# A hybrid mLSTM and sparse-attention block on one core: new pacing of background work, shared banks for turned tiles, part of the weight splits on GpSimd, and an interleaved tail

## The chip, the cores and the metric

The kernel runs on one core of a Trainium2 chip, as one launch. The metric is the time of the program on the device in microseconds. The engines are named as the profile names them: PE is TensorE, DVE is VectorE, ACT is ScalarE, POOL is GpSimd, SP is the engine that issues most DMAs.

## The reference

One decoder block on x of 512 tokens by 1024 channels, in float32:

```
u    = rmsnorm(x, norm_in)
proj = u @ w_in                                  # 1024 x 6736, split into the parts below
# mLSTM group: 4 heads, q and k 128 wide (conv of 4 taps, SiLU), v 256 wide
hm   = mlstm(q, k, v, log_i, log_sigmoid(f));  hm = rmsnorm per head * m_norm
hm   = sigmoid(m_o) * hm * silu(m_z)
# attention group: 8 heads of 64; an indexer's score picks the 128 best keys of each query
score[t, s] = sum_h w[t, h] * relu(iq[t, h] . ik[s]),  s <= t;  idx = top_k(score, 128)
ha   = softmax(aq . ak / 8 + rel_bias, over idx) @ av * silu(a_z)
h    = x + concat(hm, ha) @ w_out                # 1536 x 1024
h    = h + (p @ w_ple) * sigmoid(h @ w_ple_gate) # 256 x 1024 and 1024 x 1024
out  = rmsnorm(h, norm_final)
```

## The kernel before

**Products.** Each float32 operand is split into a high part, rounded to the type that PE takes, and a low part, the rest; a product is three matmuls (high by high, high by low, low by high) into one PSUM bank. For weights, `split` (L143) does this: a slab of 1024 elements a partition (two k tiles of 512 columns, or four of 256) is loaded to `raw`, two ACT operations copy its halves to `wh`, and two DVE operations subtract to `wl`. `work` (L156) emits one of these four jobs at a tick and issues the load of a later slab when the last is out; `feed` and `piece` (L164, L172) make sure that a slab is split one slab ahead. Slabs are numbered in the order of `plan`: 36 and 37 are the columns of the first pair of attention heads, 38 to 41 the attention's v (`av`), 42 to 47 the other pairs, 48 to 51 its gate (`az`), 52 to 63 the output projection (`wo`), 64 to 73 the last products.

**Order.** The order of instructions on PE, DVE, ACT and POOL is the order in which the program emits them. A `tick` (L188) follows every step of three matmuls of a dense product. It emits what `later(n, ...)` (L182) put off until now, one weight job, and background work: `back` is a list of generators, and each tick adds 1.0 to a credit from which every piece subtracts the cost that it yields. The background holds, in this order, the indexer's scores (24 pieces, COST_SC), the gate sequences, the convolutions of q and k (COST_CV), and the top-k (48 pairs of MAX8 and MATCH_REPLACE8, L567 and L569, COST_TK a pair); `split_mix` (COST_MX) joins during the mLSTM.

**Stages.** The dense products of q and k take 64 ticks, v 64, the output gates `o` and `z` of half the mLSTM 64. The mLSTM's 32 steps are then woven (L269) with 112 steps of dense products: `gates_oz(1)`, pair 0 of the attention's q and k (`aqk`), and `av`. When the top-k has ended, the attention's 32 units (one head, one tile of 128 queries) are woven with pairs 1 to 3, `az` and most of the output projection's first half. Then come the rest of that projection, the turned residual, and the gate of the per-layer embedding (`wg`).

**PSUM.** Dense products use a ring of four banks ("mm"), everything else a second ring of four ("x"). A tile takes the bank of the tile allocated four before it in its ring, and its first write waits until that one's last reader is done. In the attention a head allocates four logits (`lg_ps`, read by `least`, L801), four turned probability tiles (`pt_ps`, L825, one for each query tile, read by a copy on ACT and a subtraction on DVE), and one product with v (`av_ps`, read last by DVE into `ha`). The turned tiles of units 0 and 1 of a head are made in the same iteration. After pair 0, the four banks of `av` follow those of `z` and of `aqk`: the third takes the query bank, the fourth the key bank, whose four subtractions (`ak2`, L776) come 2 to 5 ticks after its last matmul, the copies (`ak1`, L775) 0 to 3 ticks after it.

**Masks.** The mask of unit k+1 is added one unit ahead (L783): by POOL for all but its last 256 columns, by DVE for those.

**Tail.** `gated` (L964) evacuates a row tile of `wg`: tanh on ACT, two DVE steps that add the gated embedding to `h`, a square on ACT with an accumulated sum. `evac_gate1` (L990) does it for the second half of the columns, in two halves of 256, then the power on POOL, the multiplication by the gain, the scaling on DVE and ACT, and the stores. Row tiles 0 and 1 are made together, then 2, then 3 in two banks:

```
    for i in range(2):
        done = evac_gate1(i, [two[i], two[i]])
        later(2 + 2 * i, finish, done, 0)
        later(3 + 2 * i, finish, done, 1)
    for i in range(2, NT):
        ...
            next(done)
        run(done)
```

Of the kernel before, what the change touches and what calls it, by code (L numbers as in the profile page):

```python
# [16 lines left out]
OP = mybir.AluOpType  # L17
# [3 lines left out]
P = 128  # L21
# [9 lines left out]
DPLE = 256  # L31
EPS = 1e-6
NTMP, NHM, NKEEP = 7, 3, 37
COST_SC, COST_CV, COST_TK, COST_MX, RATE_M, RATE_A = 1.7, 2.0, 2.6, 2.0, 3.5, 3.2
NR, NW, NS = 3, 4, 1
QK0 = 10
POOLW = (0, 1, 2)
# [10 lines left out]
def block_kernel(ctx: ExitStack, tc: tile.TileContext, x, p, w_in, b_gate, conv_w, w_out, norm_in,  # L48
# [30 lines left out]
    def x_bank(name, shape=(P, S)):  # L79
        return pp.tile(list(shape), F32, tag="x", bufs=4, name=name)  # L80
# [4 lines left out]
    def f(ap):  # L85
        return ap.bitcast(F32)
# [56 lines left out]
    def split(k):  # L143

        raw = loaded.pop(k)
        nk, n = raw.shape[1:]
        h = wp.tile([P, KP * S], F32R, tag="wh", bufs=NW, name="wh")[:, 0:nk * n].rearrange("p (k n) -> p k n", n=n)
        l = wp.tile([P, KP * S], F32R, tag="wl", bufs=NW, name="wl")[:, 0:nk * n].rearrange("p (k n) -> p k n", n=n)
        ready[k] = h, l
        halves = [slice(0, nk // 2), slice(nk // 2, nk)]  # L150
        jobs.extend((k, A.activation, (h[:, q, :], raw[:, q, :], AF.Copy)) for q in halves)
        jobs.extend((k, V.tensor_tensor, (l[:, q, :], raw[:, q, :], f(h)[:, q, :], OP.subtract)) for q in halves)

    jobs = []

# [21 lines left out]

    back, credit, clock, due = [], [0.0], [0], []  # L180

    def later(n, fn, *args):  # L182
        heapq.heappush(due, (clock[0] + n, len(order), fn, args))
        order.append(None)
# [3 lines left out]
    def tick():  # L188
        clock[0] += 1
        while due and due[0][0] <= clock[0]:  # L190
            _, _, fn, args = heapq.heappop(due)
            fn(*args)  # L192
        if jobs:
            work()
        credit[0] += 1.0
        while back and credit[0] >= 0.0:
            g = back[0]
            cost = next(g, None)
            if cost is None:
                back.remove(g)  # L200
            else:
                credit[0] -= cost
        if not back:
            credit[0] = 0.0
# [430 lines left out]
    def gates_oz(c):  # L635
        yield from dense_fm(4, evac_o(4 * c), name="o")
        yield from dense_fm(4, evac_z(4 * c), name="z")
# [124 lines left out]
    def evac_aqk(pair):  # L762
        def go(b, ps):
            half = [slice(0, 64), slice(64, 128)]
            for s in range(2):
                h, me, other = 2 * pair + s, half[s], half[1 - s]
                if b == 0:
                    t = aq[h] = keep(f"aq{h}", F32R)
                    later(s, A.activation, t[me, :], ps[me, :], AF.Copy, 0.0, -DH ** -0.5)
                    later(s + 2, V.scalar_tensor_tensor, t[other, :], ps[me, :], -DH ** -0.5, f(t[me, :]),  # L770
                          OP.mult, OP.subtract)
                else:
                    t1, t2 = ak1[h], ak2[h] = keep(f"ak1_{h}", F32R), keep(f"ak2_{h}", F32R)
                    for q, o in enumerate((me, other)):
                        later(2 * s + q, A.activation, t1[o, :], ps[me, :], AF.Copy)  # L775
                        later(2 * s + q + 2, V.tensor_tensor, t2[o, :], ps[me, :], f(t1[me, :]), OP.subtract)  # L776
        return go

    def attention():
# [35 lines left out]
        def turned(t, i):  # L815
            return bass.AP(tensor=t.tensor, offset=t.offset + P * i, ap=[list(t.ap[0]), [3 * P, i + 1], [1, P]])

        def flip(h, i):
            if i == 0:
                pt[h] = [sp.tile([P, SW], F32R, tag=n, bufs=1, name=n) for n in ("sH", "sL")]  # L820
            tH, tL = pt[h]
            pr = prob.pop((h, i))
            ps = x_bank("pt_ps", (P, i + 1, P))
            for j in range(i + 1):
                T.transpose(ps[:, j, :], pr[:, j * P:(j + 1) * P], ident)  # L825
            later(1, A.activation, turned(tH, i), ps, AF.Copy)
            later(2, V.tensor_tensor, turned(tL, i), ps, f(turned(tH, i)), OP.subtract)

        def values(h):
            tH, tL = pt.pop(h)  # L830
# [20 lines left out]
        n = len(units)  # L851
        turns_at, values_at = {}, {}
        for k, (h, i) in enumerate(units):
            turns_at.setdefault(k + (4 if i == 0 else 3), []).append((h, i))
        for h in range(AH):
            values_at[NT * h + 8] = h
        masks(*units[0])
        for k in range(NT * AH + 5):
            if k < n:
                logits(*units[k])  # L860
            if k + 1 < n:
                later(1, masks, *units[k + 1])
            if k in values_at:
                h = values_at[k]
                values(h)
                if h % 2:
                    later(4 if h > 3 else 48 if h == 1 else 24, close, h // 2)
            for h, i in turns_at.get(k, ()):
                flip(h, i)
            yield  # L870


    def attention_in(b):
        return dense_fm(2, evac_aqk(b), name="aqk")
# [18 lines left out]

    tz = load_bias()
    for k, _ in enumerate(gates_oz(0)):
        if k == QK0:
            split_qk(0)
        if k == QK0 + 12:
            decays_load(0, 0)
            decays_load(0, 1)  # L900
        if k == QK0 + 18:
            decays(0, 0)
    weave(mlstm(), chain(gates_oz(1), attention_in(0), dense_tm(u_h, u_l, list(range(KT)), evac_av, name="av")),
          lambda k: RATE_M)
    while not ended[0]:
        tick()
    out0 = project(0)
    weave(attention(), chain(attention_in(1), attention_in(2), attention_in(3), dense_fm(4, evac_az, name="az"),
                             (next(out0) for _ in range(40))), lambda k: RATE_A)
# [51 lines left out]
    gfin = [gf[:, c * S:(c + 1) * S] for c in range(2)]  # L961
    fs = [col(f"fs{i}", 4) for i in range(NT)]

    def gated(i, c, ps, o, n, acc, wait):  # L964

        sg = tmp("sgg", shape=(P, n))
        t = hs[i, c][:, o:o + n]
        A.activation(sg, ps[:, o:o + n], AF.Tanh, scale=0.5)  # L968

        def add():  # L970
            V.scalar_tensor_tensor(sg, sg, 1.0, ple[i, c][:, o:o + n], op0=OP.add, op1=OP.mult)  # L971
            V.scalar_tensor_tensor(t, sg, 0.5, t, op0=OP.mult, op1=OP.add)
            if wait:
                later(2, square)
            else:
                square()

        def square():
            A.activation(sg, t, AF.Square, scale=D ** -0.5, accum_out=acc)

        if wait:
            later(1, add)
        else:
            add()

    def evac_gate0(i, ps):
        gated(i, 0, ps, 0, S, fs[i][:, 0:1], True)
        later(4, V.tensor_tensor, hs[i, 0], hs[i, 0], gfin[0], OP.mult)

    def evac_gate1(i, parts):  # L990

        r = fs[i][:, 3:4]
        for q, ps in enumerate(parts):
            gated(i, 1, ps, q * 256, 256, fs[i][:, 1 + q:2 + q], False)
            if q == 0:
                V.tensor_scalar(r, fs[i][:, 1:2], fs[i][:, 0:1], EPS, op0=OP.add, op1=OP.add)
            yield
        V.tensor_tensor(r, r, fs[i][:, 2:3], OP.add)
        G.tensor_tensor(r, r, neghalf[:, 0:1], OP.pow)
        V.tensor_tensor(hs[i, 1], hs[i, 1], gfin[1], OP.mult)  # L1000
        for q in range(2):
            cs = slice(q * 256, (q + 1) * 256)
            V.tensor_scalar(hs[i, 1][:, cs], hs[i, 1][:, cs], r, None, op0=OP.mult)
            A.activation(hs[i, 0][:, cs], hs[i, 0][:, cs], AF.Copy, scale=r)
            if i == NT - 1:
                nc.sync.dma_start(out[0, i * P:(i + 1) * P, S + q * 256:S + (q + 1) * 256], hs[i, 1][:, cs])
        if i < NT - 1:
            nc.sync.dma_start(out[0, i * P:(i + 1) * P, S:], hs[i, 1])
        nc.scalar.dma_start(out[0, i * P:(i + 1) * P, 0:S], hs[i, 0])
        yield  # L1010

# [17 lines left out]
        T.matmul(ps[:, cs], h_l(kt, i), h[:, kt % KP, cs], start=False, stop=(kt == KT - 1))  # L1029
        tick()  # L1030

    def finish(done, q):
        next(done)
        if q:
            run(done)

    two = [mm_bank(f"wg{i}") for i in range(2)]
    for k0 in range(0, KT, KP):
        for i in range(2):
            for k in range(KP):  # L1040
                gate_step(i, two[i], slice(0, S), k0 + k)
    for i in range(2):
        done = evac_gate1(i, [two[i], two[i]])
        later(2 + 2 * i, finish, done, 0)
        later(3 + 2 * i, finish, done, 1)
    for i in range(2, NT):
        parts = [mm_bank(f"wg{i}_{q}") for q in range(2 if i == NT - 1 else 1)]
        w = S // len(parts)
        done = evac_gate1(i, [parts[0], parts[-1]])
        for q, ps in enumerate(parts):  # L1050
            for kt in range(KT):
                gate_step(i, ps, slice(q * w, (q + 1) * w), kt)
            next(done)
        run(done)


def _bucket_table():
# [32 lines left out]
```

## Time and profile before

| | |
|---|---|
| time, median of 3 runs | 535.02 us (534.21 to 535.66) |
| profiled execution, its own time | 534.46 us |
| its span | 532.7 us |
| busy: PE, DVE, ACT, POOL | 500.9 (94%), 362.2 (68%), 267.2 (50%), 47.8 us (9%) |
| mean granted clock of PE | 0.984 |
| DMA | 52.25 MB, mean 98 GB/s |

The span is the stretch from the first to the last recorded work of the profiled execution; its own time is 1.8 us longer. Busy times are those of each engine's instructions; a busy PE is counted with the modelled ends of pipelined matmuls, so the distance between two starts tells more of its speed than a duration does. The rows of the next section but one give start and duration in microseconds; what stands in brackets is how long the engine had been idle before the instruction, and what released it.

### The profile page before, as it was taken

How to read it: one execution, taken by the hardware profiler on the slowest of the kernel's cores; microseconds unless marked ns; L12 is line 12 of the kernel's file. 1: busy time of each engine (PE TensorE's matmuls, PEld its weight loads, DVE VectorE, ACT ScalarE, POOL GpSimd, SP SyncE). 2: the span in 40 equal slices, each digit the busy share in tenths (PEclk: the TensorE clock that was granted, in tenths of full speed). 3: DMA queues.
4: the chain of work that ended last, by engine and by line, in shares of the span. 5: the costliest groups of instructions: out<-in, count | busy, mean ns of one | idle time of the engine just before them, and what ended most of it. 6: DMA issues, size and time to landing. Idle time of an engine off the chain costs nothing.

```text
span 532.7 us, 6811 instructions
## 1 busy us (share of the span) xinstructions
PE 500.9 (94%) x2370; PEld 409.6 (77%) x2370; DVE 362.2 (68%) x802; ACT 267.2 (50%) x588; POOL 47.8 (9%) x96
## 2 busy tenths in 40 slices
PE   5999999999999999999979999899999999999980
PEld 4887888788788878887868887678888888788770
DVE  1953464987859699879995997886983542715554
ACT  6643656552614245645654577775764332414343
POOL 4400000000000002110111211111110000000011
PEclk9999999999999999999979999999999999999996
DMA  8442553233433133341322212212234533141122
GB/s 263 141 141 53 89 113 103 81 119 119 160 112 119 43 92 113 95 124 46 100 69 79 81 40 80 79 41 79 53 113 153 172 112 111 53 145 41 39 79 79
DMA packets 37281, 52.25 MB, mean 98 GB/s; under 512 B 4156, under 2 KB 16732, under 8 KB 37248
## 3 DMA queue, kind: packets, MB, share of 16 engines
q1 hardware_dynamic: 32192, 45.49, 26.9%
q10 hardware_dynamic: 4960, 6.31, 5.5%
q8 instruction: 18, 0.29, 0.2%
q14 instruction: 15, 0.12, 0.1%
q0 software_dynamic: 96, 0.02, 0.0%
HBM read 48.13 MB, written 3.69 MB: 97 GB/s over the span
## 4 chain that ended last, share of the span: by engine, by line
PE 78%; DVE 11%; ACT 5%; issue 3%; DMA 1%; POOL 1%; SPq 0%; POOLq 0%; ACTq 0%; DVEq 0%
PE wo L256 4%; PE wo L258 4%; PE wo L257 4%; PE mv L257 3%; PE mv L256 3%; PE mv L258 3%; PE o L236 2%; PE o L234 2%; PE o L235 2%; PE z L234 2%; PE z L236 2%; PE z L235 2%; DVE wl L159 2%; DVE ak L192 2%; PE mq L234 1%
## 5 line engine op out<-in xcount | busy, mean ns | idle before, releaser
L159 DVE TENSOR_TENSOR wl<-raw,wh 128x512 fp32r<-128x512 f32 x140 | 92.9, 684 | 13.5 <-ACT wh L159 13.3
L159 ACT ACTIVATE wh<-raw 128x512 fp32r<-128x512 f32 x140 | 83.2, 624 | 16.6 <-DMA raw<-in_w_ple_gate_dram 5.7
L256 PE MATMUL wo<-wh,mixH 128*128 128x512 f32 x96 | 39.4, 410 | 0.0
L258 PE MATMUL wo<-wh,mixL 128*128 128x512 f32 x96 | 37.8, 394 | 0.0
L257 PE MATMUL wo<-wl,mixH 128*128 128x512 f32 x96 | 37.8, 393 | 0.0
L567 DVE MAX8 m<-sc 128x8 f32<-128x256 f32 (+2 forms) x48 | 26.5, 553 | 0.0
L234 PE MATMUL aqk<-uH,wh 128*128 128x512 f32 x64 | 26.5, 413 | 0.0
L236 PE MATMUL o<-uH,wl 128*128 128x512 f32 x64 | 25.5, 399 | 0.9 <-DVE wl L159 0.9
L236 PE MATMUL aqk<-uH,wl 128*128 128x512 f32 x64 | 25.4, 397 | 1.0 <-DVE wl L159 1.0
L569 DVE MATCH_REPLACE8 sc<-m,sc 128x256 f32<-128x256 f32 (+2 forms) x48 | 26.0, 542 | 0.0
L234 PE MATMUL o<-uH,wh 128*128 128x512 f32 x64 | 25.9, 404 | 0.0
L234 PE MATMUL z<-uH,wh 128*128 128x512 f32 x64 | 25.8, 403 | 0.0
L257 PE MATMUL mv<-wl,uH 128*128 128x512 f32 x64 | 25.7, 401 | 0.0
L235 PE MATMUL o<-uL,wh 128*128 128x512 f32 x64 | 25.4, 396 | 0.0
L235 PE MATMUL z<-uL,wh 128*128 128x512 f32 x64 | 25.3, 396 | 0.0
L236 PE MATMUL z<-uH,wl 128*128 128x512 f32 x64 | 25.3, 396 | 0.0
L256 PE MATMUL mv<-wh,uH 128*128 128x512 f32 x64 | 25.3, 395 | 0.0
L235 PE MATMUL aqk<-uL,wh 128*128 128x512 f32 x64 | 25.3, 395 | 0.0
L258 PE MATMUL mv<-wh,uL 128*128 128x512 f32 x64 | 25.1, 393 | 0.0
L809 ACT ACTIVATE pr<-pr,sm 128x128 f32<-128x128 f32 (+3 forms) x32 | 17.9, 560 | 13.9 <-DVE sm L801 13.6
L543 DVE SCALAR_TENSOR_TENSOR sc<-relu,iwt,sc 128x256 f32<-128x256 f32 (+2 forms) x21 | 13.0, 617 | 15.7 <-ACT relu L192 15.4
L971 DVE SCALAR_TENSOR_TENSOR sgg<-sgg,ple 128x256 f32<-128x256 f32 (+1 forms) x12 | 6.1, 508 | 23.6 <-ACT sgg L968 23.4
(244 smaller groups left out, 1354.0 us busy)
## 6 DMA issues: line engine op xcount, KB each, us to landing
raw<-in_w_in_dram SPq DMA_DIRECT2D x44, 512.0 KB, 3.5
raw<-in_w_out_dram SPq DMA_DIRECT2D x12, 512.0 KB, 3.5
raw<-in_w_in_dram SPq DMA_DIRECT2D x16, 256.0 KB, 2.9
raw<-in_w_ple_gate_dram SPq DMA_DIRECT2D x8, 512.0 KB, 3.7
x<-in_x_dram SPq DMA_DIRECT2D x8, 256.0 KB, 4.8
xr<-in_x_dram SPq DMA_DIRECT2D x2, 1024.0 KB, 4.9
tdram<-tv ACTq DMA_DIRECT2D x1, 1536.0 KB
tz<-tdram ACTq DMA_DIRECT2D x1, 1024.0 KB
```

What stands on the lines that cost most here:

```text
L159: fn(*args)
L192: fn(*args)
L234: T.matmul(banks[b][:, 0:nt], h[:, k, bs], uH[:, kt, tok0:], start=(kt == 0), stop=False)
L235: T.matmul(banks[b][:, 0:nt], h[:, k, bs], uL[:, kt, tok0:], start=False, stop=False)
L236: T.matmul(banks[b][:, 0:nt], l[:, k, bs], uH[:, kt, tok0:], start=False, stop=(kt == KT - 1))
L256: T.matmul(banks[i], aH(kt, i), h[:, k, :], start=first, stop=False)
L257: T.matmul(banks[i], aH(kt, i), l[:, k, :], start=False, stop=False)
L258: T.matmul(banks[i], aL(kt, i), h[:, k, :], start=False, stop=last)
L543: V.scalar_tensor_tensor(sc, r, w, sc, op0=OP.mult, op1=OP.add)
L567: V.max(out=m8, in_=sel[i])
L569: V.match_replace(out=sel[i], in_to_replace=m8, in_values=sel[i], imm_value=-3e38)
L809: later(2, lambda: A.activation(t, t, AF.Exp, bias=sm[:, 0:1], scale=-1.0, accum_out=sm[:, 1:2]))
```

## The change

- The costs of the background pieces fall: scores 1.7 to 1.2, convolution 2.0 to 1.6, a pair of the top-k 2.6 to 2.0. A tick adds `pace[0]` to the credit instead of 1.0: 1.0 until step 32 of `gates_oz(0)`, 0.6 to the end of it, 0.8 through the mLSTM, 1.0 afterwards.
- The low parts of the slabs 40, 42, ... 60 are subtracted on GpSimd instead of VectorE.
- The subtractions `ak2` come two ticks later.
- Turned tiles that are made in the same iteration share one bank; the copies and subtractions of each stay separate.
- In the tail the evacuation of a row tile is put off in pieces by ticks. Row tile 0 begins it before row tile 1's last two steps, the second column half is evacuated in one piece of 512 for tiles 0 to 2, the scaling by the row factor and the gain is one operation on DVE, and the last square is a DVE reduction.

```
-COST_SC, COST_CV, COST_TK, COST_MX, RATE_M, RATE_A = 1.7, 2.0, 2.6, 2.0, 3.5, 3.2
+COST_SC, COST_CV, COST_TK, COST_MX, RATE_M, RATE_A = 1.2, 1.6, 2.0, 2.0, 3.5, 3.2
+SPLITP = range(40, 62, 2)
...
-        jobs.extend((k, V.tensor_tensor, (l[:, q, :], raw[:, q, :], f(h)[:, q, :], OP.subtract)) for q in halves)
+        E = G if k in SPLITP else V
+        jobs.extend((k, E.tensor_tensor, (l[:, q, :], raw[:, q, :], f(h)[:, q, :], OP.subtract)) for q in halves)
...
-        credit[0] += 1.0
+        credit[0] += pace[0]
...
-                        later(2 * s + q + 2, V.tensor_tensor, t2[o, :], ps[me, :], f(t1[me, :]), OP.subtract)
+                        later(2 * s + q + 4, V.tensor_tensor, t2[o, :], ps[me, :], f(t1[me, :]), OP.subtract)
...
+        def flip(h, tiles):
+            if tiles[0] == 0:
                 pt[h] = [sp.tile([P, SW], F32R, tag=n, bufs=1, name=n) for n in ("sH", "sL")]
             tH, tL = pt[h]
+            ps = x_bank("pt_ps", (P, sum(tiles) + len(tiles), P))
+            o = 0
+            for i in tiles:
+                pr = prob.pop((h, i))
+                for j in range(i + 1):
+                    T.transpose(ps[:, o + j, :], pr[:, j * P:(j + 1) * P], ident)
+                part = ps[:, o:o + i + 1, :]
+                later(1, A.activation, turned(tH, i), part, AF.Copy)
+                later(2, V.tensor_tensor, turned(tL, i), part, f(turned(tH, i)), OP.subtract)
+                o += i + 1
...
     for k, _ in enumerate(gates_oz(0)):
+        if k == 32:
+            pace[0] = 0.6
...
+    pace[0] = 0.8
     weave(mlstm(), chain(gates_oz(1), attention_in(0), dense_tm(u_h, u_l, list(range(KT)), evac_av, name="av")),
           lambda k: RATE_M)
     while not ended[0]:
         tick()
+    pace[0] = 1.0
...
+    def soft(i, c, ps, o, n):
         sg = tmp("sgg", shape=(P, n))
+        A.activation(sg, ps[:, o:o + n], AF.Tanh, scale=0.5)
+        return sg
+
+    def add(sg, i, c, o, n):
         t = hs[i, c][:, o:o + n]
+        V.scalar_tensor_tensor(sg, sg, 1.0, ple[i, c][:, o:o + n], op0=OP.add, op1=OP.mult)
+        V.scalar_tensor_tensor(t, sg, 0.5, t, op0=OP.mult, op1=OP.add)
+
+    def square(sg, i, c, o, n, acc):
+        A.activation(sg, hs[i, c][:, o:o + n], AF.Square, scale=D ** -0.5, accum_out=acc)
...
+    def factor(i):
+        r = fs[i][:, 3:4]
+        V.tensor_scalar(r, fs[i][:, 0:1], fs[i][:, 1:2], EPS, op0=OP.add, op1=OP.add)
+        G.tensor_tensor(r, r, neghalf[:, 0:1], OP.pow)
+
+    def store(i):
+        r = fs[i][:, 3:4]
+        A.activation(hs[i, 0], hs[i, 0], AF.Copy, scale=r)
+        V.scalar_tensor_tensor(hs[i, 1], hs[i, 1], r, gfin[1], op0=OP.mult, op1=OP.mult)
+        nc.sync.dma_start(out[0, i * P:(i + 1) * P, S:], hs[i, 1])
+        later(1, nc.scalar.dma_start, out[0, i * P:(i + 1) * P, 0:S], hs[i, 0])
+
+    def evac_gate1(i, ps):
+        sg = soft(i, 1, ps, 0, S)
+        later(1, add, sg, i, 1, 0, S)
+        later(3, square, sg, i, 1, 0, S, fs[i][:, 1:2])
+        later(4, factor, i)
+        later(6, store, i)
+
+    def evac_last(i, parts):
+        r, w = fs[i][:, 3:4], S // 2
+        for q, ps in enumerate(parts):
+            o = q * w
+            sg = soft(i, 1, ps, o, w)
+            if q == 0:
+                later(1, add, sg, i, 1, o, w)
+                later(2, square, sg, i, 1, o, w, fs[i][:, 1:2])
+                later(3, V.tensor_scalar, r, fs[i][:, 1:2], fs[i][:, 0:1], EPS, OP.add, OP.add)
+                yield
             else:
+                add(sg, i, 1, o, w)
+                t = hs[i, 1][:, o:]
+                V.tensor_tensor_reduce(sg, t, t, 1.0 / D, 0.0, OP.mult, OP.add, fs[i][:, 2:3])
+                V.tensor_tensor(r, r, fs[i][:, 2:3], OP.add)
         G.tensor_tensor(r, r, neghalf[:, 0:1], OP.pow)
...
     for k0 in range(0, KT, KP):
         for i in range(2):
             for k in range(KP):
                 gate_step(i, two[i], slice(0, S), k0 + k)
+            if k0 + KP == KT:
+                evac_gate1(i, two[i])
...
+        if q:
+            while due:
+                _, _, fn, args = heapq.heappop(due)
+                fn(*args)
+        next(done)
```

## Rows read from the trace of the kernel before

**Rows 1.** Windows: start:end, length, busy of PE, PEld, DVE, ACT, POOL, clock, DMA.
```profile
93.50:138.50 45.00, 44.97 (x193) 35.62 (x192) 37.17 (x60) 20.88 (x36) 0.21 (x2) 1.00 0.29 94
138.70:161.80 23.10, 23.10 (x104) 18.18 (x103) 16.43 (x33) 9.18 (x18) 0.59 (x2) 1.00 0.49 161
...
185.00:297.00 112.00, 106.84 (x532) 88.58 (x531) 97.21 (x241) 59.63 (x152) 15.26 (x30) 0.97 0.30 86
297.00:360.00 63.00, 58.64 (x291) 48.13 (x290) 53.73 (x146) 45.14 (x104) 9.26 (x11) 1.00 0.22 68
...
518.00:532.70 14.70, 0.00 (x0) 0.00 (x0) 6.50 (x18) 4.78 (x15) 1.86 (x2) 0.65 0.27 100
```

**Rows 2.** Waits of PE, whole span: us in total, times, longest.
```profile
PE av L256 <- DVE ak L192: 3.2, 1, 3.2
PE pt_ps L825 <- DVE sm L801: 2.2, 1, 2.2
PE pt_ps L825 <- DVE ha L192: 2.0, 3, 1.1
...
PE aqk L236 <- DVE wl L159: 1.0, 1, 1.0
```

**Rows 3.** Timeline of PE at `av`: start, us, instruction, idle before.
```profile
270.71 0.76 PE L256 MATMUL av<-wh,uH 128*128 128x512 f32 x1 [3.22 <-DVE ak L192]
271.27 0.63 PE L257 MATMUL av<-wl,uH 128*128 128x512 f32 x1
271.70 0.63 PE L258 MATMUL av<-wh,uL 128*128 128x512 f32 x1
```

**Rows 4.** Window of the 6 us after that wait.
```profile
272.00:278.00 6.00, 6.00 (x20) 4.90 (x20) 5.68 (x14) 3.63 (x7) 0.30 (x1) 0.60 0.37 101
```

**Rows 5.** Timeline of the tail: PE, ACT, DVE, POOL.
```profile
517.63 0.28 PE L1029 MATMUL wg<-wh,hL 128*128 128x256 f32 x1
...
517.52 0.39 ACT L968 ACTIVATE sgg<-wg 128x256 f32<-128x256 f32 x1 [0.42 <-ACT h L1004]
...
525.39 0.36 ACT L968 ACTIVATE sgg<-wg 128x256 f32<-128x256 f32 x1
...
529.38 0.34 ACTq L1009 DMA_DIRECT2D out_dram<-h  x1
...
525.78 0.42 DVE L971 SCALAR_TENSOR_TENSOR sgg<-sgg,ple 128x256 f32<-128x256 f32 x1
...
527.48 0.93 POOL L999 TENSOR_TENSOR fs<-fs,neghalf 128x1 f32<-128x1 f32 x1 [5.19 <-DVE fs L998]
```

**Rows 6.** The page's costliest groups: count, busy us, mean ns of one, idle before.
```profile
L159 DVE TENSOR_TENSOR wl<-raw,wh 128x512 fp32r<-128x512 f32 x140 | 92.9, 684 | 13.5 <-ACT wh L159 13.3
L159 ACT ACTIVATE wh<-raw 128x512 fp32r<-128x512 f32 x140 | 83.2, 624 | 16.6 <-DMA raw<-in_w_ple_gate_dram 5.7
...
L567 DVE MAX8 m<-sc 128x8 f32<-128x256 f32 (+2 forms) x48 | 26.5, 553 | 0.0
...
L569 DVE MATCH_REPLACE8 sc<-m,sc 128x256 f32<-128x256 f32 (+2 forms) x48 | 26.0, 542 | 0.0
```

**Rows 7.** Timeline of DVE ahead of the wait at `av`.
```profile
265.84 0.69 DVE L192 TENSOR_TENSOR ak<-aqk,ak 64x512 fp32r<-64x512 f32 x1 [0.66 <-ACT ak L192]
...
269.15 0.69 DVE L567 MAX8 m<-sc 128x8 f32<-128x512 f32 x1
269.87 0.69 DVE L192 TENSOR_TENSOR ak<-aqk,ak 64x512 fp32r<-64x512 f32 x1
```

**Rows 8.** Groups of POOL by shape: weight splits at the kernel's start.
```profile
L334 POOL TENSOR_TENSOR wl<-raw,wh 128x512 fp32r<-128x512 f32 x3 | 4.3, 1430 | 2.0 <-ACT wh L333 2.0
```

**Rows 9.** Timeline at the kernel's start: DVE, then POOL.
```profile
14.05 0.69 DVE L346 TENSOR_TENSOR uL<-u,uH 128x512 fp32r<-128x512 f32 x1
...
21.42 1.43 DVE L346 TENSOR_TENSOR uL<-u,uH 128x512 fp32r<-128x512 f32 x1
...
20.79 2.16 POOL L410 TENSOR_TENSOR ml<-mraw,mh 128x608 fp32r<-128x608 f32 x2 [2.74 <-ACT mh L409]
```

More of the change, by code (lines that the diff above doesn't have):

```diff
@@ L176, in piece @@
         return ready.pop(k)
-    back, credit, clock, due = [], [0.0], [0], []
+    back, credit, clock, due, pace = [], [0.0], [0], [], [1.0]
     def later(n, fn, *args):
@@ L816, in turned @@
             return bass.AP(tensor=t.tensor, offset=t.offset + P * i, ap=[list(t.ap[0]), [3 * P, i + 1], [1, P]])
-        def flip(h, i):
-            if i == 0:
+        def flip(h, tiles):
+            if tiles[0] == 0:
                 pt[h] = [sp.tile([P, SW], F32R, tag=n, bufs=1, name=n) for n in ("sH", "sL")]
             tH, tL = pt[h]
[L822 to L827, printed above, removed]
+            ps = x_bank("pt_ps", (P, sum(tiles) + len(tiles), P))
[8 more added lines that the diff above has]
+                o += i + 1
         def values(h):
@@ L853, in attention @@
         for k, (h, i) in enumerate(units):
-            turns_at.setdefault(k + (4 if i == 0 else 3), []).append((h, i))
+            turns_at.setdefault(k + (4 if i == 0 else 3), (h, []))[1].append(i)
         for h in range(AH):
@@ L867, in attention @@
                     later(4 if h > 3 else 48 if h == 1 else 24, close, h // 2)
-            for h, i in turns_at.get(k, ()):
-                flip(h, i)
+            if k in turns_at:
+                flip(*turns_at[k])
             yield
@@ L962, in block_kernel @@
     fs = [col(f"fs{i}", 4) for i in range(NT)]
-    def gated(i, c, ps, o, n, acc, wait):
+    def soft(i, c, ps, o, n):
         sg = tmp("sgg", shape=(P, n))
+        A.activation(sg, ps[:, o:o + n], AF.Tanh, scale=0.5)
+        return sg
+    def add(sg, i, c, o, n):
         t = hs[i, c][:, o:o + n]
[L968 to L974, printed above, removed]
-            else:
[L976 to L998, printed above, removed]
+        V.scalar_tensor_tensor(sg, sg, 1.0, ple[i, c][:, o:o + n], op0=OP.add, op1=OP.mult)
@@ new lines, in add, with evac_gate0 @@
+        V.scalar_tensor_tensor(t, sg, 0.5, t, op0=OP.mult, op1=OP.add)
+    def square(sg, i, c, o, n, acc):
+        A.activation(sg, hs[i, c][:, o:o + n], AF.Square, scale=D ** -0.5, accum_out=acc)
+    def evac_gate0(i, ps):
+        sg = soft(i, 0, ps, 0, S)
+        later(1, add, sg, i, 0, 0, S)
+        later(3, square, sg, i, 0, 0, S, fs[i][:, 0:1])
+        later(5, V.tensor_tensor, hs[i, 0], hs[i, 0], gfin[0], OP.mult)
+    def factor(i):
+        r = fs[i][:, 3:4]
+        V.tensor_scalar(r, fs[i][:, 0:1], fs[i][:, 1:2], EPS, op0=OP.add, op1=OP.add)
+        G.tensor_tensor(r, r, neghalf[:, 0:1], OP.pow)
@@ L999, in evac_gate1 @@
         G.tensor_tensor(r, r, neghalf[:, 0:1], OP.pow)
-        V.tensor_tensor(hs[i, 1], hs[i, 1], gfin[1], OP.mult)
         for q in range(2):
-            cs = slice(q * 256, (q + 1) * 256)
-            V.tensor_scalar(hs[i, 1][:, cs], hs[i, 1][:, cs], r, None, op0=OP.mult)
+            cs = slice(q * w, (q + 1) * w)
+            V.scalar_tensor_tensor(hs[i, 1][:, cs], hs[i, 1][:, cs], r, gfin[1][:, cs], op0=OP.mult, op1=OP.mult)
             A.activation(hs[i, 0][:, cs], hs[i, 0][:, cs], AF.Copy, scale=r)
-            if i == NT - 1:
-                nc.sync.dma_start(out[0, i * P:(i + 1) * P, S + q * 256:S + (q + 1) * 256], hs[i, 1][:, cs])
@@ L1007, in evac_gate1 @@
-        if i < NT - 1:
-            nc.sync.dma_start(out[0, i * P:(i + 1) * P, S:], hs[i, 1])
+            nc.sync.dma_start(out[0, i * P:(i + 1) * P, S + q * w:S + (q + 1) * w], hs[i, 1][:, cs])
         nc.scalar.dma_start(out[0, i * P:(i + 1) * P, 0:S], hs[i, 0])
@@ L1030, in gate_step @@
         tick()
[L1032 to L1035, printed above, removed]
     two = [mm_bank(f"wg{i}") for i in range(2)]
@@ L1041, in block_kernel @@
                 gate_step(i, two[i], slice(0, S), k0 + k)
[L1042 to L1054, printed above, removed]
+            if k0 + KP == KT:
+                evac_gate1(i, two[i])
+    ps = mm_bank("wg2")
+    for kt in range(KT):
+        gate_step(2, ps, slice(0, S), kt)
+    evac_gate1(2, ps)
+    parts = [mm_bank(f"wg3_{q}") for q in range(2)]
+    done = evac_last(3, parts)
+    for q, ps in enumerate(parts):
+        for kt in range(KT):
+            gate_step(3, ps, slice(q * S // 2, (q + 1) * S // 2), kt)
+        if q:
[3 more added lines that the diff above has]
+        next(done)
 def _bucket_table():
```

## The prediction

> **What bounds the kernel now.** I read the page first: PE is busy 94% of the span of 532.7 us, so only time in which PE stands idle or runs at the lower clock can be won, unless matmuls are removed, and the change removes none. The table of windows by stage shows where that is [rows 1]. The reader is to compare the first two numbers of each row: PE is full in the v and o stages (93.5 to 161.8), loses 5.2 us in the mLSTM stage (112.00 against 106.84), 4.4 us at the start of the attention (63.00 against 58.64), and does nothing in the last 14.7 us. DVE is the engine that is nearly full beside it: 97.21 of 112, 53.73 of 63.
>
> The waits of PE name what ends its idle time [rows 2]. One wait of 3.2 us is for `ak`, the split of pair 0's keys; 4.2 us in four waits are transposes of the attention (`pt_ps`) that wait for a PSUM bank which DVE has still to read, through `least` (L801, `sm`) or `ha`. The remaining waits are about 1 us each, for a weight's low part `wl`. The 3.2 us has a second cost: from 270.71 to 276.9 the 512-column matmuls begin 0.43 us apart [rows 3] instead of the 0.23 of elsewhere, some 14 of them: 2.8 us. [...] After the 2.2 us wait the matmuls kept their 0.23.
>
> **The tail.** PE's last matmul ends at 517.9 and the span at 532.7 [rows 5]. In between, the evacuations of the row tiles run as one serial chain: the first `sgg` of tile 2 is at 517.52, tile 3's second half starts at 525.39, 7.5 us after its matmuls were done, and needs 7.3 us to the end. Were it free to start with PE's end, the gain would be 7.5 us. The new order interleaves the tiles, yet ScalarE still meets tile 2's whole chain before tile 3's. I lay it out with 0.62 us for a 128x512 operation on ACT and 0.69 on DVE [rows 6], 0.42 and 0.4 for 128x256, 0.95 for the power on POOL, 0.34 for a DMA issue on ACT [rows 5]. Tile 2's bank is complete at 512.0 on the old time axis; ACT is then busy with tile 1's store until about 512.9. Tanh 0.62, two DVE steps 1.38, square with its accumulator read 0.8, factor 0.2, power 0.95, scaled copy 0.62, DMA issue 0.34, small hand-overs 0.2: 518.0. Tile 3's first half follows on ACT: tanh 0.4, add 0.9, square 0.6, sum 0.2: its second half starts at 520.0 instead of 525.39. That is 5.4 us. The second half itself is as long as before: the square moves from ACT to DVE (one 128x256 operation each, without the hand-over and back), the separate multiplication by the gain goes but lay beside the power, and two fused 128x256 operations (0.84) take the place of 0.62 for the scaling, beside ACT's two scaled copies of 0.5 each. Ends: 4.8 (another hand-over late) to 7.5. I take **-5.4**.
>
> **Pacing of the top-k.** Each tick is one step of three matmuls and adds credit; a background piece subtracts its cost. Before: prepare 15, scores 24 x 1.7, sequences 17, conv 8 x 9, gate columns 7 make 151.8, so the top-k starts at tick 152; its 48 pairs cost 124.8 and 3 more, the split of the mLSTM output 24, and it ends at tick 303.6 of the 304 at which the mLSTM stage ends. After: 15 + 28.8 + 17 + 59.2 = 120, so it starts at tick 121; 40 ticks at 1.0, 32 at 0.6 (the gate's z stage), then 0.8, and 99 + 7 + 16 to pay: it ends at about tick 270, that is 78 ticks into the mLSTM. A pair costs DVE 1.1 us [rows 6]. Counted by stage in pairs: v stage 0 then 4, o stage 3.5 then 12.5, z stage 12 then 10, mLSTM to tick 248 18.5 and 18.5, after tick 248 15.5 then 4.5. So DVE is relieved of 11 pairs, 12 us, exactly in the stretch with `ak` and `av` (ticks 256 to 304), and pays in v and o.
>
> What that costs there: v stage 37.2 us of 45 [rows 1], with four pairs and four more conv steps, less the scans that move ahead: about 42. o stage 16.4 of 23.1, with nine pairs more and 5.5 us of conv less: about 21. Both stay under PE's time, but a weight's low part has only some four ticks (2.8 us) from issue to use. I charge +0.3, between 0 and 3. The waits of about 1 us at `o` and `aqk` lie before tick 260, where the density of pairs is the same: nothing won.
>
> **The `ak` subtraction, two ticks later.** Before tick 304 the fourth `av` bank is pair 0's key bank, and PE reached it at 267.49 and waited to 270.71 [rows 3]. DVE's rows show why: the last `ak` stands behind top-k pieces (a MAX8 of 0.69, and a replacement with a load before it), and the second of the four follows an idle 0.66 us in which it waited for ACT, itself waiting for the `ak` before [rows 7]. After the change the four ACT copies come first and the four subtractions after them, the last one issued in the very step ahead of the matmul that needs it. What is queued behind is little; the DVE is free of the top-k by then. ACT's fourth copy ends near 266.3 (it has a square and a weight half ahead), then DVE owes two gates, one `wl` and two subtractions: about 268.9, a wait of 1.4 instead of 3.2. That is shorter than the 2.2 us that left the clock alone, so the 2.8 us come back too: **-4.6**. Ends: 0 (the later issue eats what the top-k gives) to -6.0. The same two ticks apply to pair 3 before `az`, whose fourth bank has no wait now: +0.7, with 0 and +1.5 as ends.
>
> **One bank for two turned tiles.** Per head the ring of four banks now serves nine tiles: four logits, four turned, one `av_ps`. In the chain of waits the tile of i=1 follows the logits of one unit before, and that of i=2 follows `av_ps` of the same unit's neighbour. With eight tiles the roles fall on fixed pairs: i=2 after the logits of the unit before, the logits two units later after `av_ps`, the rest two units or more apart. The 2.0 us on `ha` go, and the 2.2 on `sm` become a wait on an older bank [rows 2]. What is late next is DVE itself: if it is 2 us behind, i=2 meets the unfinished `least`. I leave 0.8 of 4.4 there.
>
> **Low parts on GpSimd.** 11 weight slabs, 22 halves. Each takes 0.68 us from DVE [rows 6] and 1.43 on POOL [rows 8]; two halves are 2.9 us of the 8 to 9 us that a slab lasts in the attention, and POOL is busy 9.3 us of 63 there [rows 1]. Behind them in POOL's queue stand the masks of rows i > 1 (0.9 us each), which run a unit ahead. In the stalled stretch four slabs fall on POOL: 5.5 us less of DVE's 53.7. The price is what DVE loses while POOL reads: at the start of the kernel a `uL` subtraction took 0.69 us alone and 1.43 beside POOL's 2.16 us [rows 9], so from 0 to 0.74 for each half, 0 to 5.9 us here. I take 2, since most of DVE's operations there read one operand from PSUM; the relief left (3.5 us) is what makes the bank change count. The three parts together: **-2.9** (-4.4 + 0.8 + 0.7), ends +1.5 and -4.4. POOL's slab at tick 283 stands ahead of a decay's mask: +0.3, from 0 to 1. In the projections PE is full and POOL has 5.6 us a slab: 0.
>
> [...]
>
> **Sum.** -5.4 - 4.6 - 2.9 + 0.3 + 0.3 = -12.3. The profiled execution took 534.46 us, 1.8 around its span; 534.46 - 12.3 = **522.2**. The median shown is 535.02, 0.6 above that execution, within the runs' own spread.
>
> **Rivals.** (A) the forecast, 518.5 to 525: 0.60. (B) The waits only move: the last `ak` is issued too late for its matmul, 3.2 us and the slow clock stay, and the transposes wait for `least`: 522.2 + 4.6 to 7.5 = 526.8 to 529.7. For it: the issue moved to the last possible step; against: 11 pairs less. 0.20. (C) POOL and DVE block each other for whole operations: 16 halves in the attention cost 16 x 1.43 = 22.9 us for 10.9 removed, 12 us more of DVE in 116 us that have 25 free; the attention keeps its 4.4 us and adds about 2 (522.2 + 2.9 + 2): 527 to 530. For it [rows 9], against it that few operations there have two SBUF inputs. 0.08. (D) slower: the o stage is the place. If DVE, held in order by `wl` halves that wait for ACT, cannot use its 2 us of slack, every slab's low part is late; a wait over 3 us also brings the slow clock at 2.8 us each. Three such (3 x 6 = 18 us) outweigh the 12.3: 540. Decides from 12 us of lag on; against: 21 of 23.1. 0.05. (E) all waits go, and the 1 us ones too: 534.46 - 6.5 - 6.0 - 4.4 - 2 = 515.6: 0.07.
>
> The range 516.5 to 529.5 leaves out D, the far end of C and of E. Faster than before by over 0.3% (1.6 us, about what a measurement of this kernel can tell): A, B, C, E less a little, 0.93; within 0.3% 0.02; slower 0.05.
>
> **What would show it.** Tail: the time from the last matmul to the span's end near 9.4 us instead of 14.8, tile 3's last tanh some 2 us after PE's end. Pacing: the last MAX8 about 25 us before the first logits, PE at `av` waiting under 2 us, no window with a clock below 1.00 before the tail. Attention: no `pt_ps` wait on `ha`, under 1.5 us on DVE altogether, POOL's `wl` near 1.4 us, DVE's busy time down by some 13 us. Wrong: PE waits for `wl` in the o stage, a wait of 3 us at `av` or `az`, or more than 11 us after the last matmul.

## The result and the profile after

The changed kernel takes 527.62 us (median, 526.09 to 529.75) against 535.34 for the kernel before on the same chip: ratio 0.9862, 95% interval 0.9824 to 0.9900. The forecast was 522.2, its range 516.5 to 529.5. So it is faster and inside the range, but by 7.7 us instead of 12.3, and it lies where rival B was put (526.8 to 529.7). The profiled execution took 527.67 us with a span of 525.1.

The windows of the kernel after, as in [rows 1] (the last one begins with the end of PE's last matmul):

```profile
93.50:138.50 45.00, 45.00 (x194) 36.21 (x193) 37.55 (x63) 20.32 (x35) 0.10 (x1) 1.00 0.30 95
138.70:161.80 23.10, 23.10 (x103) 18.37 (x103) 22.26 (x58) 8.09 (x17) 1.73 (x2) 1.00 0.54 172
185.00:297.00 112.00, 108.46 (x541) 90.06 (x540) 87.43 (x210) 60.68 (x156) 23.24 (x36) 0.97 0.31 90
297.00:360.00 63.00, 57.94 (x280) 47.55 (x279) 50.06 (x131) 42.91 (x101) 18.15 (x16) 0.97 0.19 59
517.30:525.10 7.80, 0.00 (x0) 0.00 (x0) 2.95 (x9) 1.69 (x5) 0.55 (x1) 0.69 0.31 113
```

Two things are to be seen. DVE did what the pacing asked: 22.26 us busy in the o stage instead of 16.43, 87.43 in the mLSTM stage instead of 97.21, and PE is full in v and o. But PE's idle time in the attention did not fall: 63.00 against 57.94, 5.1 us, where it was 4.4. And from the last matmul to the end it is 7.8 us instead of 14.8. PE's last matmul ends at 517.26; before it was 517.91. So the tail gave 7 us of the span, and all the rest together 0.65.

The waits of PE in the kernel after, as in [rows 2]:

```profile
PE av L258 <- DVE ak L194: 2.9, 1, 2.9
PE az L236 <- DVE ak L194: 2.6, 1, 2.6
PE pt_ps L829 <- DVE sm L803: 2.2, 1, 2.2
...
PE aqk L238 <- DVE wl L161: 0.5, 1, 0.5
```

The wait at `av` is nearly what it was, 2.9 for 3.2, although the top-k is gone; one of 2.6 us at `az` is new; the transposes' waits on `ha` are gone, the one on `sm` is not. The timeline of PE at both, and windows of what follows each:

```profile
268.28 0.77 PE L258 MATMUL av<-wh,uH 128*128 128x512 f32 x1 [2.92 <-DVE ak L194]
...
352.59 0.48 PE L236 MATMUL az<-uH,wh 128*128 128x512 f32 x1 [2.63 <-DVE ak L194]
```
```profile
268.30:274.50 6.20, 6.20 (x17) 5.04 (x18) 3.52 (x8) 2.83 (x6) 1.81 (x2) 0.50 0.16 48
...
352.60:360.00 7.40, 7.40 (x28) 6.03 (x29) 4.15 (x14) 3.24 (x8) 2.56 (x2) 0.77 0.03 10
```

The slow clock, a granted clock below 1.00, came after each: 0.50 from 268.30 to 274.50 and 0.77 from 352.60 to 360.00. Why the wait at `av` stayed is in the timelines of ACT and DVE ahead of it, in the same kernel, `ak` alone:

```profile
258.80 1.19 ACT L194 ACTIVATE ak<-aqk 64x512 fp32r<-64x512 f32 x2
...
260.84 0.59 ACT L194 ACTIVATE ak<-aqk 64x512 fp32r<-64x512 f32 x1
...
262.51 0.59 ACT L194 ACTIVATE ak<-aqk 64x512 fp32r<-64x512 f32 x1
...
263.14 0.68 DVE L194 TENSOR_TENSOR ak<-aqk,ak 64x512 fp32r<-64x512 f32 x1 [0.39 <-ACT ak L194]
...
264.55 0.69 DVE L194 TENSOR_TENSOR ak<-aqk,ak 64x512 fp32r<-64x512 f32 x1
...
266.00 0.69 DVE L194 TENSOR_TENSOR ak<-aqk,ak 64x512 fp32r<-64x512 f32 x1
...
267.44 0.69 DVE L194 TENSOR_TENSOR ak<-aqk,ak 64x512 fp32r<-64x512 f32 x1
```

The first subtraction needs only the first copy, done by 259.4, yet it starts at 263.14, when the fourth copy ends. DVE reached it only shortly before, since it is issued four ticks after the keys' last matmul, and then stood 0.39 us waiting for ACT. All four subtractions then follow at 1.4 us each, since a weight half, another weight half and a state product are issued between them. PE was there at 265.36; the last subtraction ends at 268.13. At `az` it is the same with pair 3's keys: the fourth copy ends at 346.33, the last subtraction runs from 351.75 to 352.44, and PE was there at 349.96.

```profile
345.75 0.58 ACT L194 ACTIVATE ak<-aqk 64x512 fp32r<-64x512 f32 x1
...
351.75 0.69 DVE L194 TENSOR_TENSOR ak<-aqk,ak 64x512 fp32r<-64x512 f32 x1
```

### The profile page after: what moved, and what is told of

Its sections match the earlier page's. It is cut to its first block, busy times and chain, and to the rows that moved or that the text cites. A ratio compares the mean times of both kernels' runs of the same rounds, so it can differ in the third digit from the quotient of the medians.

```text
span 525.1 us, 6781 instructions
## 1 busy us (share of the span) xinstructions
PE 500.9 (95%) x2370; PEld 410.3 (78%) x2370; DVE 353.8 (67%) x766; ACT 265.1 (50%) x574; POOL 77.4 (15%) x118
## 4 chain that ended last, share of the span: by engine, by line
PE 76%; DVE 12%; ACT 5%; issue 3%; DMA 1%; POOL 1%; SPq 0%; POOLq 0%; ACTq 0%; DVEq 0%
PE wo L258 4%; PE wo L260 4%; PE wo L259 4%; PE mv L260 3%; PE mv L259 3%; PE mv L258 3%; PE o L238 2%; PE o L236 2%; PE o L237 2%; PE z L236 2%; PE z L238 2%; PE z L237 2%; DVE wl L161 2%; DVE ak L194 2%; PE mq L236 1%
## 5 line engine op out<-in xcount | busy, mean ns | idle before, releaser
L161 DVE TENSOR_TENSOR wl<-raw,wh 128x512 fp32r<-128x512 f32 x118 | 78.6, 684 | 5.1 <-ACT wh L161 4.9
L161 POOL TENSOR_TENSOR wl<-raw,wh 128x512 fp32r<-128x512 f32 x22 | 29.2, 1336 | 91.2 <-issue 57.2
L671 POOL TENSOR_SCALAR_AFFINE_SELECT e<-e 128x128 f32<-128x128 f32 x16 | 6.8, 426 | 119.4 <-DMA e<-adram 116.4
```

Source lines behind the costliest of these rows:

```text
L671: G.affine_select(out=e[:, 0:P], in_=e[:, 0:P], compare_op=OP.is_ge, fill=-BIG, base=0, pattern=[[1, P]], channel_multiplier=-1)
```

## The experiments

**One part undone: the subtractions at 2 to 5 ticks again.**

```
-                        later(2 * s + q + 4, V.tensor_tensor, t2[o, :], ps[me, :], f(t1[me, :]), OP.subtract)
+                        later(2 * s + q + 2, V.tensor_tensor, t2[o, :], ps[me, :], f(t1[me, :]), OP.subtract)
```

> The changed kernel with one part undone: the subtractions ak2 come 2 to 5 ticks after the last matmul of the keys again, not 4 to 7. Theory 1 (the two ticks cost it): copies on ACT and subtractions on DVE of one bank run one after the other in the order of issue, so with the late issue the first subtraction starts only after the fourth copy (263.1 on the time axis of the changed kernel) and then stands between weight splits on DVE. Undone, PE's wait at av falls from 2.9 to under 1.5 us, the one at az from 2.6 to under 1 us, the granted clock is 1.00 in both places, and the time falls by 6 to 9 us, to about 520. Rival (DVE is simply late there, whatever the order): the waits stay within 0.7 us of 2.9 and 2.6 and the time within 2 us of 527.6.

517.45 us (ratio to before 0.9674, 0.9655 to 0.9692): 10.2 us under the whole change. PE's waits in this kernel:

```profile
PE pt_ps L829 <- DVE sm L803: 1.5, 2, 0.8
...
PE av L258 <- DVE ak L194: 0.2, 1, 0.2
```

The wait at `az` is gone. The first two subtractions of pair 0 now stand between the copies, and the last one ends at 265.14, 3.0 us earlier:

```profile
260.00 0.67 DVE L194 TENSOR_TENSOR ak<-aqk,ak 64x512 fp32r<-64x512 f32 x1
...
264.45 0.69 DVE L194 TENSOR_TENSOR ak<-aqk,ak 64x512 fp32r<-64x512 f32 x1
```

The clock is 1.00 in every stage before the tail, and the same 2370 matmuls take PE 496.5 us instead of 500.9. So the two ticks cost 2.7 us at `av`, 2.6 at `az`, 0.7 at `pt_ps` and 4.4 of slow clock: 10.4 of the 10.6 us between the two spans (525.1 and 514.5). Theory 1 holds; the gain is above its 6 to 9.

**The tail alone.** The changed kernel with everything but the tail put back:

```
-COST_SC, COST_CV, COST_TK, COST_MX, RATE_M, RATE_A = 1.2, 1.6, 2.0, 2.0, 3.5, 3.2
-SPLITP = range(40, 62, 2)
+COST_SC, COST_CV, COST_TK, COST_MX, RATE_M, RATE_A = 1.7, 2.0, 2.6, 2.0, 3.5, 3.2
+SPLITP = ()
...
-                        later(2 * s + q + 4, V.tensor_tensor, t2[o, :], ps[me, :], f(t1[me, :]), OP.subtract)
+                        later(2 * s + q + 2, V.tensor_tensor, t2[o, :], ps[me, :], f(t1[me, :]), OP.subtract)
...
-                flip(*turns_at[k])
+                for i in turns_at[k][1]:
+                    flip(turns_at[k][0], [i])
...
-            pace[0] = 0.6
+            pace[0] = 1.0
...
-    pace[0] = 0.8
+    pace[0] = 1.0
```

> The kernel before with the new tail alone: old costs and pace, subtractions on DVE, own banks, ak2 at 2 to 5 ticks. Theory 1: the tail gives 7 us by itself (7.8 us from the last matmul to the end instead of 14.8) and the rest of the change nothing net, so the time is 527 to 529, the same as the whole change within 1.5 us. Rival (the middle wins a good part, and the tail only some 5 us): 529 to 531, 2 us or more above the whole change.

529.07 us (0.9881, 0.9854 to 0.9908), 5.8 us under before and 1.5 above the whole change. That lies at the edge of both, just above theory 1's 527 to 529 and at the low end of the rival's 529 to 531, and the intervals of the two kernels overlap: it does not decide between them.

**Without GpSimd's share, and without the shared bank**, both with the late subtractions. The edits are `SPLITP = ()` and the loop over `flip` shown above.

> The changed kernel with all low parts on DVE again. Theory 1 (POOL's share is worth little, since the two long waits are set by the order of the key's copies): DVE busy rises by 12 to 15 us, the time stays within 2 us of the changed kernel. Rival a (the relief is needed): the attention's waits grow and the time rises by 3 to 5 us. Rival b (POOL and DVE block each other): DVE's operations with two SBUF inputs get shorter, the time falls by 2 us or more.

> The changed kernel with a bank of its own for every turned tile. Theory 1: waits of pt_ps on ha come back (about 2 us in all) beside the 2.2 us on sm, time up by 1 to 3 us. Rival (DVE is late anyway, the bank only says where PE waits): the sum of PE's waits in the attention is the same within 1 us, and so is the time.

528.01 (0.9874, 0.9853 to 0.9894) and 527.88 us (0.9866, 0.9843 to 0.9889): neither differs from 527.62. Without POOL's share the time stays where theory 1 had it, against both rivals; DVE is busy 360.5 us instead of 353.8, half of the rise that theory 1 gave. With own banks the wait at `az` is only 0.7, but `pt_ps` waits 3.1 us on `ha` and 1.8 on `sm`: as long as DVE is late with the keys, PE's time is lost at one bank or another. That was the rival's claim.

**The same two without the late subtractions**, from the kernel of 517.45 us.

> The changed kernel with ak2 at 2 to 5 ticks and all low parts on DVE. Theory 1 (with the keys' order out of the way, DVE's load in the attention sets the rest): DVE busy up by 8 to 10 us, PE's waits in the attention up from 1.5 to about 3 us, time 518.5 to 520. Rival (POOL's share is worth nothing also here): within 0.8 us of 517.5.

> The changed kernel with ak2 at 2 to 5 ticks and a bank of its own for every turned tile. Theory 1 (the ring of banks sets what is left): waits of pt_ps on ha of 1.5 to 2.5 us come back, time 518.5 to 520.5. Rival (a bank more or less only moves the wait): within 0.8 us of 517.5.

POOL's share: 518.03 (0.9693, 0.9672 to 0.9715), 0.6 us more, no difference that this can tell; DVE's busy time rose by 7.8 us, and PE's waits in the attention by 0.5. The rival was right. The shared bank: 521.82 (0.9751, 0.9726 to 0.9775), 4.4 us more, so it is worth more than theory 1 said: 3.5 us of waits in the attention instead of 1.8, and the one of 1.95 us that ends at 329.20 is followed by a slow clock (0.72 from 329.20 to 335.20; PE busy 498.0 us instead of 496.5). These two make 3.2 us. PE's two waits for the load of x at the start differ by another 1.2 us between these two profiles, and are 1.2 to 2.5 us in all profiled executions: a difference of about 1 us between two kernels is not to be read as the worth of a part.

```profile
PE pt_ps L829 <- DVE sm L803: 1.9, 1, 1.9
PE pt_ps L829 <- DVE ha L194: 1.6, 2, 1.0
```
```profile
329.20:335.20 6.00, 6.00 (x23) 4.91 (x24) 4.44 (x14) 4.76 (x13) 1.52 (x2) 0.72 0.30 87
```

**Old pacing with the early subtractions; and the late ones alone in the kernel before.**

> The changed kernel with ak2 at 2 to 5 ticks and, beside it, the old costs and a pace of 1.0 throughout. Theory 1 (new pacing and the early issue are both needed at av: the top-k has to be out of DVE's queue): the wait of 3.2 us at av comes back with the slow clock after it, about 6 us, and the time is 522 to 525. Rival (the early issue alone would do, with tail, banks and POOL): at av under 1.5 us and 517 to 519.

> The kernel before with one part of the change: ak2 at 4 to 7 ticks. Theory 1 (the late issue costs by itself): the wait at av is 4 us or more instead of 3.2, one of 0.5 to 2.6 us appears at az, and the time rises by 1 to 4 us to 536 to 539. Rival (with the top-k in the queue, or without it, the two ticks don't matter there): 534 to 535.5 and 3.2 us at av.

524.67 (0.9814, 0.9796 to 0.9833): the 3.2 us at `av` are back, as theory 1 had it, and the pacing is worth 7.2 us. 539.47 (1.0083, 1.0062 to 1.0104): the two ticks alone make the kernel before 4.8 us slower, just above theory 1's 536 to 539, with this wait, and 0.6 at `az`:

```profile
PE av L256 <- DVE ak L192: 5.4, 1, 5.4
```

**The pacing and the tail alone** (own banks, no POOL share, early subtractions), for the sum.

> The kernel before with the new tail and the new costs and pace alone: ak2 at 2 to 5 ticks, own banks, low parts on DVE. Theory 1 (the parts add up: own banks cost 4.4 us, POOL's share is worth 0.6, against 517.45 with all of them): 522 to 523, some 6.5 us under the tail alone (529.07), from the 3.2 us at av and the slow clock after it. Rival (the relief of DVE by POOL matters once the banks are apart): 524 to 526.

522.32 (0.9768, 0.9745 to 0.9791). With the early subtractions the parts add up: without the shared bank and POOL's share together it is 4.9 us more than 517.45, where the two alone were 4.4 and 0.6. In one order: tail alone 529.1, with the pacing 522.3, with the shared bank 518.0, with POOL 517.5; the two ticks bring it back to 527.6.

**How the bank is shared.** Three kernels differ from that of 517.45 us in one number of ticks.

> The changed kernel with all four copies ak1 issued at tick 0 and the subtractions at 2 to 5 ticks. Theory 1 (two engines take turns at one bank in the order of issue): the first subtraction of pair 0 starts only after the fourth copy, 2.4 us after the first copy began, against 1.4 us with two copies ahead, and its wait names ACT's ak; the subtractions then follow without a wait for ACT, the last one ends no later than with 2 to 5 ticks, and the time is within 1.5 us of 517.5. Rival (a subtraction waits for its own copy alone): the first subtraction starts as early as with two copies ahead, 1.4 us after the first copy began.

Here the copies are issued with `later(0, ...)`. 519.19 us (0.9697, 0.9677 to 0.9716); ACT and DVE:

```profile
259.41 2.40 ACT L194 ACTIVATE ak<-aqk 64x512 fp32r<-64x512 f32 x4
...
261.84 1.38 DVE L194 TENSOR_TENSOR ak<-aqk,ak 64x512 fp32r<-64x512 f32 x2 [0.91 <-ACT ak L194]
...
265.43 0.69 DVE L194 TENSOR_TENSOR ak<-aqk,ak 64x512 fp32r<-64x512 f32 x1
```

The first subtraction starts at 261.84, 2.43 us after the first copy began and as the fourth ends, and waited 0.91 us for ACT's `ak`: the order of issue at the bank rules, not the own copy. The wait at `av` stays at 0.3. The time is 1.7 us above, a little more than said; PE waits 1.0 us more at `av_ps` and 0.4 more at `pt_ps`, and the kernel before took 0.8 us more beside this one than beside that of 517.45 us.

> The changed kernel with ak2 at 3 to 6 ticks, halfway. Theory 1 (order of issue at one bank: copy, copy, copy, then subtraction and fourth copy in turn): the wait at av lies between 0.2 us (2 to 5 ticks) and 2.9 (4 to 7), about 1.3, too short for the slow clock; the one at az between 0 and 2.6; time about 519 to 521. Rival (a threshold, nothing between): either 517.5 or 527.6 within 1 us.

520.17 us (0.9709, 0.9690 to 0.9728): 1.5 us at `av` and 1.2 at `az`, the clock 1.00 after both. It lies between, as theory 1 had it.

> The changed kernel with each ak2 issued in the same tick as its ak1: 0 to 3 ticks, so copies and subtractions alternate at the bank. Theory 1 (the chain of eight at one bank, 4 x 0.6 + 4 x 0.69 = 5.2 us, only has to begin early): no wait at av or az, what is left of pt_ps at or under 1.5 us, time 516 to 518. Rival (DVE stalled in order by copies that are late now holds up other work): waits of pt_ps rise by over 1 us, time above 518.5.

521.41 us (0.9738, 0.9716 to 0.9759). No wait at `av` or `az`, but 2.5 us at `av_ps` and 0.9 at `pt_ps`. DVE and ACT now wait for each other in turn: three of pair 0's four subtractions stood 0.66 to 1.00 us idle for a copy, one copy 1.56 for a subtraction. Theory 1's time was wrong, the rival's right, though at another tile: `pt_ps` waits less, not more. Of the four delays tried (0, 2, 3 and 4 ticks), 2 is the best.

## Why the prediction was right in sign and wrong in size

**The step that failed is the one of the `ak` subtraction**, -4.6 forecast. I wrote that the four copies come first, and still let only two of the four subtractions stand behind the fourth copy, with the last one's end 2.6 us after it. All four stood behind it (the row at 263.14), with other work of DVE between them, and the last one ended 5.0 us after the fourth copy. The copy ended 3.2 us earlier than I had put it (263.1 for 266.3) and PE came 2.1 us earlier (265.36 for 267.49), which took 1.1 off the wait: 1.4 + 2.4 - 1.1 = 2.7, and with 0.15 from the subtraction's end to PE's start the 2.9 measured. So the slow clock did not go either: 2.7 us of it followed. The same step put +0.7 at `az`, with +1.5 as the end: it was 2.6 us and 1.7 of slow clock. Rival B had named the mechanism ("issued too late for its matmul") at 0.20; the kernel before with the late issue alone (539.47 us) shows that it holds there too.

That the time still lies inside the range is in part luck. The two terms of the keys were to give 3.9 us together and cost 3.9 instead (waits and slow clock of 6.0 us before, 9.9 after). Against that stand 1.6 us more from the tail, and PE's waits for a weight's `wl` from DVE, which fell from 2.5 us to under 1 where the forecast had charged 0.3. Of the forecast's own signs, a wait under 2 us at `av`, no clock below 1.00 before the tail, under 1.5 us at `pt_ps` and 13 us less of DVE's time (8.4 measured) did not come true; at `av` and `az` it came close to the wait of 3 us that I had called wrong.

**The tail** was mis-sized the other way: 7.0 us of span, not 5.4. The rows of ACT and POOL after, as in [rows 5]:

```profile
511.54 0.60 ACT L976 ACTIVATE sgg<-wg 128x512 f32<-128x512 f32 x1 [0.47 <-PE wg L1055]
...
516.42 0.39 ACT L976 ACTIVATE sgg<-wg 128x256 f32<-128x256 f32 x1 [0.45 <-ACT h L1001]
...
518.17 0.36 ACT L976 ACTIVATE sgg<-wg 128x256 f32<-128x256 f32 x1
...
521.71 0.37 ACTq L1035 DMA_DIRECT2D out_dram<-h  x1
...
520.19 0.55 POOL L1029 TENSOR_TENSOR fs<-fs,neghalf 128x1 f32<-128x1 f32 x1 [4.97 <-DVE fs L1028]
```

The chain is the one that I laid out, tile 2 and then tile 3 on ACT, but it starts 0.7 us earlier against PE and its powers take 0.55 us instead of 0.93: the last tanh is at 518.17, 0.9 us after PE's end instead of the 2 forecast. Part of the 7.0 us is given back outside the span: 2.6 us of the profiled execution's time lie around it instead of 1.8 (2.1 to 2.6 in all kernels with the new tail, 1.8 in the two with the old one). What that is, the traces don't show.

**The pacing's arithmetic** held: the last MAX8 starts at 253.10 instead of 293.83, 34 steps of the dense products earlier, as the credits say (that is 42 us ahead of the first logits, where I had put 25). DVE is busy 22.3 us in the o stage, for 21 forecast, without a wait of PE for `wl` of more than 0.1 us there, against rival D; 9.8 us less on DVE in the mLSTM stage for 12 forecast. Its worth was hidden behind the two ticks: 7.2 us with the early issue.

**The banks** did what was derived: no wait on `ha`, and the late `least` (L803) as the next thing, though with 2.2 us instead of the 0.8 that I left. With the late keys they were worth nothing (527.88 us without them), with the early ones 4.4 us, of which waits and clock show 3.2.

**Low parts on POOL** are worth 0.4 us with the late keys and 0.6 with the early ones, no difference that this can tell. The 22 halves are 15 us of DVE's time, but DVE was busy only 6.7 and 7.8 us less with them on POOL: some 0.33 to 0.38 us came back for each half, for the 0.25 that I took (2 us for eight) and rival C's 1.43. A part of it is that the attention's masks, which read two SBUF tiles, take 0.50 us in the mean instead of 0.43, and one beside POOL's two halves at 339.11 took 1.18:

```profile
339.51 1.18 DVE L791 TENSOR_TENSOR pr<-sc,tz 128x256 f32<-128x256 f32 x1
```
```profile
339.11 2.74 POOL L161 TENSOR_TENSOR wl<-raw,wh 128x512 fp32r<-128x512 f32 x2 [6.14 <-issue]
```

The masks are some 1.5 us of it; where the rest lies was not followed. A subtraction that reads `pt_ps` in PSUM took 0.54 us at 340.62, beside the second of these halves, against 0.55 in the mean of its shape (128x384); that fits the reason for which I took 2 us out of 0 to 5.9.

## What to carry to other kernels

When two engines read one PSUM bank in turns, as ACT and DVE did here (DVE waited 0.39 us at 263.14, and 0.91 at 261.84 with the copies first), a delay put on the second one's reads is paid at the bank's next tenant, and can cost more than one expects: the two ticks cost 2.7 us at `av`, one tick 1.3. Count all the reads behind the last one of the first engine, and the work issued between them. A change of several parts can hide one that costs 10 us; undoing each part once shows it. A wait of PE of some two or three microseconds is to be priced with the slow clock that may follow: here 4.4 us after the two waits of 2.9 and 2.6.

## What the runs showed of the hardware

The forecast took a wait of 2.2 us for one that leaves the clock alone. In the kernel before it did (1.00 from 336.6 to 342), but it is not so sure: at the same place, a wait of 2.15 us in the changed kernel was followed by a granted clock of 1.00 (336.7 to 342), one of 2.2 us in the kernel with the tail alone by 0.72 (337 to 340), and one of 1.95 us with own banks and early subtractions by 0.72 (329.2 to 335.2). One of 1.5 us, at `av` with the subtractions at 3 to 6 ticks, left it at 1.00. Single runs of the changed kernel, with three waits between 2.2 and 2.9 us, differ more (clocks 0.982 to 0.990, 526.09 to 529.75 us) than those of the kernel without them (0.995 to 0.996, 517.1 to 518.15 us). That may come from this; no run shows it.

POOL's power of one column took 0.93 us in the old tail, where DVE multiplied two SBUF tiles beside it, and 0.55 in the new one, where DVE waits for it. No run changed this alone. The multiplication beside the last power of the old tail (527.48 to 528.41):

```profile
527.32 0.69 DVE L1000 TENSOR_TENSOR h<-h,gf 128x512 f32<-128x512 f32 x1
```
